# High and low activation parts of a projection as one 512-column product into a whole PSUM bank

## The chip, the cores and the metric

The kernel runs on one core of a Trainium2 chip. TensorE (PE) multiplies, VectorE (DVE), ScalarE (ACT) and GpSimd (POOL) do the rest of the arithmetic, SyncE (SP) issues most transfers. Each engine works through its own queue in order; semaphores tie the queues together. The metric is the device time of one execution in microseconds (us), the median over the runs.

## The reference, cut to what matters

256 tokens of width 1024 go through two layers of a first block (attention and a convolutional feed-forward network, FFN, each) and then through one hybrid layer. All of it is float32.

```
def conv_ffn(x, w_up, conv_w, conv_b, w_down):          # twice; FFN_HIDDEN = 2816
    u = x @ w_up                                        # [256, 5632]
    c = conv_b + sum of conv_w[j] * (u shifted by j - 1 tokens), j = 0..2
    g, val = c[..., :FFN_HIDDEN], c[..., FFN_HIDDEN:]
    return (jax.nn.gelu(g) * val) @ w_down

def hybrid_layer(x, ...):
    proj = rmsnorm(x) @ w_in
    (q_a, k_a, v_a, z_a, q_b, k_b, v_b, z_b, beta, decay, gate_a, gate_b) = split(proj)
    o_a = moba_attention(rope(q_a), rope(k_a), v_a)     # 8 heads; one block of 256 keys: causal attention
    y_a = (o_a * silu(z_a)) @ w_branch_a
    q_b, k_b, v_b = silu(causal_dwconv(concat(q_b, k_b, v_b)))
    o_b = gated_deltanet(q_b, k_b, v_b, g, beta)        # 8 heads
    y_b = (rmsnorm(o_b) * silu(z_b)) @ w_branch_b
    return x + rmsnorm((sigmoid(gate_a) * y_a + sigmoid(gate_b) * y_b) @ w_out)
```

`gated_deltanet` (GDN below) solves, in each head and each chunk of tokens, a triangular system of equations before its state can be carried on.

## The kernel before, in words

**Products in two parts.** PE multiplies in fp32r, and every operand of a weight product is split into a high part (rounded) and a low part (the rest). `mm3` (L130 to L133) issues three matmuls for one product: weights high by activations high (L131), weights high by activations low (L132), weights low by activations high (L133). Each loads its weights anew. In most projections the weights are the loaded operand, 128x128, and the 256 tokens stream as 256 columns; a projection sums eight k tiles. `wload` brings weights: SP issues the transfer (L110, five buffers), ACT rounds the high part (L116), DVE subtracts to get the low part (L117).

**PSUM.** A PSUM bank holds 512 float32 columns. Four banks are accumulators, tag "acc"; the four others are given out by tag in each layer: two "sm" and two "mm" in the FFN, one "sm", two "mm" and one "s" in the hybrid layer.

**The FFN** (L564) goes over 22 column tiles j. For j of 2 and more, two up products (gate and value half) are 16 `mm3` into the lower 256 columns of two banks; ACT and DVE read these banks for the three-tap convolution (L618, L619, L621), gelu follows, and the down product of an earlier j adds into the four accumulators with 512-column matmuls.

**The hybrid layer** (L734) is one function. Written order: v_a; beta and decay; the q_b and k_b projections of eight heads ("kq", `proj2`, L866, 16 `mm3` per head into one bank, alternately "acc" and "mm"), each followed by a four-tap convolution (L855), SiLU and the sum of squares on PE (`sumsq`, L876); from these sums reciprocal norms (from L898 on); the GDN matrices (L934, L937, L948 on PE, L952 and L954 on DVE, transposed by L927 and copied by L928); a round trip over DRAM and a substitution of 15 dependent steps (L973, L974) on DVE; v_b of four head pairs; three doubling levels (L1019, with L1029 and L1035 on DVE and the transposes L1038), for four systems each (two chunks, two groups of four heads); the outputs, four heads at a time (L1054, transposes L1059); then MoBA attention head by head (projection `h_qk`, copied out by ACT at L1102, scores L1110 to L1113, transposes L173, output L1134 and L1135) with the z projections (`zproj`, L1088); and last the gates and branches (L1174 on) and the output projection.

**What sets the order.** The written order is not the order of the queues. When the program is built, a scheduler orders the instructions of every engine and gives out the buffers; an instruction that takes a bank stands behind the release of that bank's last holder. So independent MoBA work, written behind GDN, is placed between GDN's steps where its banks allow it. The helper `behind` (L187) only adds such an order between two instructions. Before, the MoBA, z, gate and branch projections use "mm" banks (one each), and GDN's levels and outputs use "acc" banks (L923).

Of the kernel before, what the change touches and what calls it, by code (L numbers as in the profile page):

```python
# [17 lines left out]
P = 128  # L18
# [19 lines left out]
def build(tc, a, out):  # L38
# [15 lines left out]
    def banks(c2, **tags):  # L54
        """four banks of a layer, by tag; the other four are accumulators"""
# [44 lines left out]
    tsl = [slice(0, P), slice(P, 2 * P)]  # L100

    def wload(src, n, part=1024, tag="w", hb=HB, pool=None, eng=None, mk=None, scale=None):
        """a weight chunk [128, n]; returns its parts as (high, low) float32r tiles"""
# [30 lines left out]

    def small(n, dt=F32, tag=None):
        return xp.tile([P, n], dt, tag=tag or f"sm{n}", name=nm("s"), bufs=4 if n <= 8 else 1)
# [3 lines left out]
    def rsqrt(v, n, mul=1.0):  # L140
        """v [P, n] (all positive) -> mul/sqrt(v): bit guess, one tuned and one cubic step."""
# [21 lines left out]
        # y1 is -1/K1 of the first step's value  # L163
# [4 lines left out]
    def tposes(src_list, dst_hi, dst_lo=None, scale=None, eng="v", tag="sm"):  # L168
        """transpose [P,128] pieces into one bank, then move to dst ([P, n, 128] view)."""
# [17 lines left out]
    def behind(*ins):  # L187
        """what is traced here goes behind these instructions on their engines"""
# [13 lines left out]
    def newton(ss, n, width, ins=False, mid=None):  # L202
        """1/sqrt(mean(x^2)+eps) from the scaled sums of one or two parts: bit guess and two Newton
        steps, the first with tuned constants; the sums come scaled so that no factor is left over."""
# [27 lines left out]
    def postnorm(pool, tb, bnk, g_bc):  # L232
        """h += rmsnorm(y) g"""
# [13 lines left out]
    def postnorm_cut(pool, tb, cut, g_bc):  # L247
        """the same for the last token block, in pieces that go out as they are done"""
# [15 lines left out]
    def prenorm(tb, g_bc, aft, warm_):  # L264
        """xT = transpose(rmsnorm(h) g) as high and low parts; 1/rms enters through the transposing product"""
        ss = small(2, F32, "ss2")
        # without a gain here it is in the weights that follow
        hg = [xp.tile([P, 512], F32, tag=f"hg{tb}{f}", name=nm("hg"), bufs=1) if g_bc is not None else h[:, tb, hf[f]] for f in range(2)]
        for f in range(2):
            j_ = square(h[:, tb, hf[f]], D, ss, f)  # L270
            if warm_:
                # keeps the clock of the tensor engine up while it waits
# [30 lines left out]

    ends = []
    gate = []

    def boundary(accs, post, pre):
        """residual add of one sublayer and the norm of the next, a token block at a time;
        returns xT and what is left to do of it, by token block"""
        xT = None  # L310
        with npool() as pool:
# [5 lines left out]
            if pre:  # L317
                xT = [xp.tile([P, KT, S], F32R, tag=f"xT{i}", name=nm("xT"), bufs=1) for i in range(2)]
# [25 lines left out]
    def wide(src4, xT, bnk, mk=None, eng=None, hold=(), k0=4, cut=False):  # L344
        """generator: bnk[tb][f] = x @ w, w [1024, 1024] in four chunks of two k tiles; a step is one k tile
# [387 lines left out]
    def hybrid(xT, fin):  # L733
        with ExitStack() as c2:  # L734
# [125 lines left out]
            def big():  # L860
                cnt[0] += 1
                return acc() if cnt[0] % 2 else mmb()
# [465 lines left out]
```

## Time and profile before

| what | us |
|---|---|
| median of 3 runs | 1037.83 |
| lowest, highest | 1037.38, 1040.54 |
| span of the profiled execution | 1037.8 |
| PE busy in it | 1012.7 (98%) |
| DVE busy | 738.0 (71%) |
| ACT busy | 545.3 (53%) |
| HBM read | 160.08 MB, 156 GB/s |

The profiled execution's span is 1037.8 us, which is the median. PE's share is the first thing to look at; next, stage by stage, what DVE and ACT do beside it, and where in the hybrid layer PE's time goes to work that waits on other engines. The stages are, in the trace: FFN of layer 0 from about 150 us, FFN of layer 1 from about 480 us, the kq projections about 677 to 723 us, the GDN matrices and substitution to 795 us, levels and outputs 795 to 860 us, then MoBA and z, and the gates and branches about 910 to 1005 us.

### The profile page before, as it was taken

What the parts mean: (1) busy time and instruction counts of PE and PEld (TensorE: products, weight loads), DVE (VectorE), ACT (ScalarE), POOL (GpSimd) and SP (SyncE); (2) the same over time, 40 slices, a digit from 0 to 9 for tenths busy, and PEclk for the clock granted to TensorE, in tenths of its full rate; (3) what the DMA queues carried; (4) which work ended last, traced back from release to release, by engine and by line L of the source; (5) the groups of instructions that cost most, each with busy time, mean ns of one, the idle gap of its engine ahead of it and who ended that gap; (6) DMA issues with size and microseconds to landing.
All of it is one profiled execution on the core that took longest, in us unless ns stands there. A gap on an engine that the chain in (4) does not pass through costs nothing.

```text
span 1037.8 us, 18147 instructions
## 1 busy us (share of the span) xinstructions
PE 1012.7 (98%) x7120; PEld 924.6 (89%) x7120; DVE 738.0 (71%) x1387; ACT 545.3 (53%) x949; POOL 33.1 (3%) x35
## 2 busy tenths in 40 slices
PE   8889899999999999999999999999999999999997
PEld 6778799999987888799999998799898999999996
DVE  5775687777668479778777767578799657685563
ACT  5653466555436456557555554465554455544451
POOL 0000100000012000010000001000203000000000
PEclk9999999999999999999999999999999999999999
DMA  7562467555325425276655442444244413455541
GB/s 276 173 219 81 168 204 222 186 185 179 124 93 189 158 100 172 88 243 234 205 185 187 156 141 76 162 162 164 81 135 102 141 54 113 160 181 185 183 163 41
DMA packets 55301, 162.70 MB, mean 157 GB/s; under 512 B 12784, under 2 KB 15280, under 8 KB 55216
## 3 DMA queue, kind: packets, MB, share of 16 engines
q1 hardware_dynamic: 55216, 161.55, 47.4%
q8 instruction: 56, 0.92, 0.3%
q14 instruction: 29, 0.24, 0.1%
HBM read 160.08 MB, written 1.44 MB: 156 GB/s over the span
## 4 chain that ended last, share of the span: by engine, by line
PE 84%; DVE 9%; ACT 3%; DMA 2%; issue 1%; SPq 0%; POOL 0%; DVEq 0%; ACTq 0%; POOLq 0%
PE mm L131 11%; PE mm L132 11%; PE mm L133 11%; PE acc L132 8%; PE acc L131 8%; PE acc L133 8%; PE sm L133 4%; PE sm L132 4%; PE sm L131 4%; PE mm L583 2%; PE acc L1019 2%; DVE lo L117 1%; PE acc L1054 1%; PE s L699 1%; ACT junk L199 1%
## 5 line engine op out<-in xcount | busy, mean ns | idle before, releaser
L117 DVE TENSOR_TENSOR lo<-raw,hi 128x1024 fp32r<-128x1024 f32 (+1 forms) x271 | 326.5, 1208 | 140.6 <-ACT hi L116 139.4
L116 ACT CAST hi<-raw 128x1024 fp32r<-128x1024 f32 (+1 forms) x271 | 278.2, 1035 | 244.6 <-PE mm L132 126.6
L133 PE MATMUL mm<-xT,lo 128*128 128x256 f32 x928 | 265.6, 286 | 0.0
L131 PE MATMUL mm<-xT,hi 128*128 128x256 f32 x928 | 265.3, 286 | 0.0
L132 PE MATMUL mm<-xT,hi 128*128 128x256 f32 x928 | 264.9, 285 | 0.0
L132 PEld LDWEIGHTS mm<-xT,hi 128*128 128x128 f32 x928 | 177.6, 191 | 1.9 <-issue 0.7
L131 PEld LDWEIGHTS mm<-xT,hi 128*128 128x128 f32 x928 | 177.5, 191 | 1.5 <-issue 0.3
L133 PEld LDWEIGHTS mm<-xT,lo 128*128 128x128 f32 x928 | 177.6, 191 | 1.3 <-issue 0.7
L131 PE MATMUL sm<-xT,hi 128*128 128x256 f32 (+1 forms) x328 | 92.8, 283 | 0.0
L133 PE MATMUL sm<-xT,lo 128*128 128x256 f32 (+1 forms) x328 | 92.8, 283 | 0.0
L132 PE MATMUL sm<-xT,hi 128*128 128x256 f32 (+1 forms) x328 | 92.8, 283 | 0.0
L131 PE MATMUL acc<-hi,gv 128*128 128x512 f32 x176 | 69.2, 393 | 0.0
L132 PE MATMUL acc<-lo,gv 128*128 128x512 f32 x176 | 69.0, 392 | 0.0
L133 PE MATMUL acc<-hi,gv 128*128 128x512 f32 x176 | 68.5, 389 | 0.0
L132 PEld LDWEIGHTS sm<-xT,hi 128*128 128x128 f32 (+1 forms) x328 | 62.2, 190 | 0.9
L131 PEld LDWEIGHTS sm<-xT,hi 128*128 128x128 f32 (+1 forms) x328 | 62.2, 190 | 0.8
L133 PEld LDWEIGHTS sm<-xT,lo 128*128 128x128 f32 (+1 forms) x328 | 62.2, 190 | 0.1
L383 ACT ACTIVATE e<-s,s 128x256 f32<-128x256 f32 x46 | 21.5, 472 | 34.6 <-DVE s L380 32.8
L133 PEld LDWEIGHTS acc<-hi,gv 128*128 128x128 f32 x176 | 33.1, 188 | 7.5 <-DVE gv L125 0.3
L131 PEld LDWEIGHTS acc<-hi,gv 128*128 128x128 f32 x176 | 33.2, 189 | 6.3 <-ACT gv L125 0.6
L132 PEld LDWEIGHTS acc<-lo,gv 128*128 128x128 f32 x176 | 33.2, 189 | 5.3
L131 PE MATMUL mm<-og,hi 128*128 128x256 f32 x128 | 36.0, 281 | 0.0
(462 smaller groups left out, 1905.0 us busy)
## 6 DMA issues: line engine op xcount, KB each, us to landing
raw<-in_ffn_up SPq DMA_DIRECT2D x88, 512.0 KB, 4.6
raw<-in_ffn_down SPq DMA_DIRECT2D x44, 512.0 KB, 4.4
raw<-in_diff_qk SPq DMA_DIRECT2D x16, 512.0 KB, 5.2
raw<-in_h_kq SPq DMA_DIRECT2D x16, 512.0 KB, 4.5
raw<-in_h_qk SPq DMA_DIRECT2D x16, 512.0 KB, 3.9
raw<-in_h_z SPq DMA_DIRECT2D x16, 512.0 KB, 3.7
raw<-in_h_gate SPq DMA_DIRECT2D x16, 512.0 KB, 4.5
raw<-in_h_br SPq DMA_DIRECT2D x16, 512.0 KB, 4.6
```

The source lines that it names most:

```text
L116: nc.scalar.copy(hi[:, :k], raw[:, :k])
L117: (eng or nc.vector).tensor_tensor(lo[:, :k], raw[:, :k], hi.bitcast(F32)[:, :k], op=ALU.subtract)
L131: nc.tensor.matmul(o, l[0], r[0], start=start, stop=False)
L132: nc.tensor.matmul(o, l[0], r[1], start=False, stop=False)
L133: return nc.tensor.matmul(o, l[1], r[0], start=False, stop=stop)
L199: nc.scalar.activation(junk[:, :p.shape[-1]], p, AF.Square, scale=math.sqrt(beta_of(width)), accum_out=ss[:, i:i + 1])
L383: nc.scalar.activation(e[:, i], s_ps[:, i], AF.Exp, bias=mx[:, i:i + 1], scale=scale, accum_out=sm[:, i:i + 1])
L583: last = nc.tensor.matmul(mmf[j][:, t, tsl[tb]], raws[j][t][:, kt * P:kt * P + P], xF[kt // 4][:, kt % 4, tsl[tb]], start=kt == 0, stop=kt ...
L699: nc.tensor.matmul(sb, q[:, tsl[tb]], kb, start=True, stop=False)
L1019: nc.tensor.matmul(b[:, i], lhs(i), rhs(i), start=True, stop=True)
L1054: nc.tensor.matmul(b[:, i], lhs(hds[i], i), rhs(hds[i], i), start=True, stop=True)
```

## The change

A projection with 256 tokens now streams the high and the low activations as one 512-column matmul behind one load of the high weights, into the two halves of a bank, and the low weights times the high activations go on top of the first half. ACT copies the second half to SBUF and DVE adds the first half to it. High and low activations lie in one tile for this (`both`).

```diff
+    def mm2(o, l, r, start, stop):
+        nc.tensor.matmul(o, l[0], r, start=start, stop=False)
+        return nc.tensor.matmul(o[:, :S], l[1], r[:, 0], start=False, stop=stop)
+
+    def halves_sum(dst, o):
+        nc.scalar.copy(dst, o[:, S:])
+        return nc.vector.tensor_tensor(dst, o[:, :S], dst, op=ALU.add)
...
+    def both(pool, name, n):
+        t = pool.tile([P, 2, n, S], F32R, tag=name, name=nm(name), bufs=1)
+        return t[:, 0], t[:, 1], t
...
-                    b = [bank("mm" if j % 2 else "sm")[:, :S] for _ in range(2)]
+                    bs_ = [bank("mm" if j % 2 else "sm") for _ in range(2)]
                     for t in range(2):
                         for kt in range(KT):
-                            mm3(b[t], [w[:, kt * P:kt * P + P] for w in wu[t]], (xT[0][:, kt], xT[1][:, kt]),
-                                kt == 0, kt == KT - 1)
+                            mm2(bs_[t], [w[:, kt * P:kt * P + P] for w in wu[t]], xT[2][:, :, kt], kt == 0, kt == KT - 1)
+                    b = lp.tile([P, 2, S], F32, tag="u", name=nm("u"), bufs=2)
+                    for t in range(2):
+                        halves_sum(b[:, t], bs_[t])
+                    b = [b[:, t] for t in range(2)]
...
-            def big():
+            def two():
                 cnt[0] += 1
-                return acc() if cnt[0] % 2 else mmb()
+                return [mmb() if cnt[0] % 3 == 0 else acc() for _ in range(2)]
...
+            def projd(w, r=xd):
+                b_ = two()
+                for t in range(2):
+                    for kt in range(KT):
+                        last_mm[:] = [mm2(b_[t], [u[:, kt * P:kt * P + P] for u in w[t]], r(kt), kt == 0, kt == KT - 1)]
+                return b_
+
+            def added(b_, dst=None):
+                if dst is None:
+                    u_ = pair(0) if og[0] else lt("w5", [P, 4, P], bufs=6).rearrange("p (t b) s -> p t (b s)", t=2)
+                else:
+                    u_ = dst
+                for t in range(2):
+                    halves_sum(u_[:, t], b_[t])
+                return u_
...
-                b = proj2(wload(a["h_kq"][hd], 2048), big)
+                b = projd(wload(a["h_kq"][hd], 2048))
                 if pend is not None:
                     with behind(*last_mm):
                         sumsq(*pend)
+                b = added(b)
...
-                b = proj2(wload(a["h_z"][br, hp], 2048))
+                b = added(projd(wload(a["h_z"][br, hp], 2048)))
...
-                b = proj2(wload(a["h_qk"][hd], 2048))
-                qk = pair(0)
-                nc.scalar.copy(qk, b)
+                b = projd(wload(a["h_qk"][hd], 2048))
+                qk = added(b, pair(0))
...
-                    b = proj2(wload(a["h_gate"][br, mp], 2048))
+                    b = added(projd(wload(a["h_gate"][br, mp], 2048)))
...
-                    b = mmb().rearrange("p (t s) -> p t s", t=2)
-                    for t in range(2):
-                        for kt in range(KT):
-                            mm3(b[:, t], [u[:, kt * P:kt * P + P] for u in w[t]], (og[br][0][:, kt], og[br][1][:, kt]), kt == 0, kt == KT - 1)
+                    b = added(projd(w, lambda kt: og[br][2][:, :, kt]))
```

`mm3` stays in the attention of both layers, in v_a, v_b, beta and decay, in the down products and in the output projection. In the hybrid layer a projection now takes two banks, two "mm" at every third and two "acc" otherwise, where it took one. Lines move: L1019 of before is L1057 after, L1038 is L1076, L876 is L913, L934, L937 and L948 are L972, L975 and L986, L927 is L965; the two matmuls of `mm2` are L138 and L139.

The scheduler gives the queues a new order. The first place is PE behind the kq projections. Before, from the last matmul of the last kq projection on (mm_7854 is its bank, acc_7959 and acc_7986 hold GDN's decay matrices, acc_7972 and acc_7979 products of keys):

```order
L133 MATMUL mm_7854<-xT_6902,lo_7851 128x256
L876 MATMUL s_7296<-ones_7010,w_1537_7761 128x1 x4
L934 LDWEIGHTS idb_7008
L934 MATMUL acc_7959<-mG_7000,idb_7008 128x512
L937 MATMUL acc_7959<-h_triu_6992,gg_7278 128x128 x4
L948 MATMUL acc_7972<-QK_7295 128x256 x2
L948 MATMUL acc_7979<-QK_7295 128x256 x2
L934 LDWEIGHTS idb_7008
L934 MATMUL acc_7986<-mG_7000,idb_7008 128x512
L937 MATMUL acc_7986<-h_triu_6992,gg_7278 128x128 x4
L131 MATMUL mm_8177<-xT_6902,hi_8167 128x256
```

After, the same first GDN matrix (acc_7433) in its surroundings; mm_7732 is the bank of the second v_b pair, and 70 matmuls of v_b stand between the last kq matmul and this place:

```order
L132 MATMUL mm_7732<-xT_6457,hi_7722 128x256
L133 MATMUL mm_7732<-xT_6457,lo_7723 128x256
L131 MATMUL mm_7732<-xT_6457,hi_7722 128x256
L972 LDWEIGHTS idb_6562
L972 MATMUL acc_7433<-mG_6554,idb_6562 128x512
L975 MATMUL acc_7433<-h_triu_6546,gg_6832 128x128 x4
L986 MATMUL acc_7446<-QK_6849 128x256 x2
```

The first matrix stood directly behind the last kq matmul, and v_b (mm_8177) began behind two of them; now v_b's first pair and part of its second stand ahead of the first matrix, and the last sums of squares (L913) stand behind 96 v_b matmuls.

The second place is PE in the doubling levels. Before, one system and the start of the next (acc_8585 and acc_8591 are the level's two products, acc_8597 the transposes, mm_9250 is a projection of another part, s_9170 a MoBA head):

```order
L1038 MATMUL acc_8578<-c_ident,A_8153 128x128 x4
L1019 MATMUL acc_8585<-A_8153,M_7958 128x64 x4
L173 MATMUL sm_9165<-c_ident,ea_9153 128x128
L131 MATMUL mm_9250<-xT_6902,hi_9246 128x256
L132 MATMUL mm_9250<-xT_6903,hi_9246 128x256
L133 MATMUL mm_9250<-xT_6902,lo_9247 128x256
L131 MATMUL mm_9250<-xT_6902,hi_9246 128x256
L1019 MATMUL acc_8591<-w_1684_8584,VT_8154 128x64 x4
L1134 MATMUL s_9170<-pTa_9164,va_7022 128x256
L1135 MATMUL s_9170<-pTa_9164,va_7022 128x128
L1038 MATMUL acc_8597<-c_ident,A_8153 128x128 x4
L1019 MATMUL acc_8604<-A_8153,M_7958 128x64 x4
```

After, from the first level product on:

```order
L1057 MATMUL acc_7964<-A_7627,M_7432 128x64 x4
L1057 MATMUL acc_7970<-w_1714_7963,VT_7628 128x64 x4
L1076 MATMUL acc_7976<-c_ident,A_7627 128x128 x4
L1057 MATMUL acc_7983<-A_7627,M_7432 128x64 x4
L1057 MATMUL acc_7989<-w_1718_7982,VT_7628 128x64 x4
L1076 MATMUL acc_7995<-c_ident,A_7627 128x128 x4
L1057 MATMUL acc_8002<-A_7627,M_7432 128x64 x4
```

It goes on so for all 24 level products, the eight groups of transposes and the 16 groups of the outputs (two L1097, fourteen L1092): nothing of another part stands between them. Ahead of them stand, since the last kq matmul, the 192 matmuls of v_b, two `h_qk` projections of 32 matmuls each (mm_8305 and mm_8306, mm_8529 and mm_8530) and the scores of one head. The first z projection (acc_8389) and the other heads' `h_qk` projections follow behind the last output.

## Rows read from the trace of the kernel before

**Rows 1.** The page: busy time, share of the span, instructions.
```profile
PE 1012.7 (98%) x7120; PEld 924.6 (89%) x7120; DVE 738.0 (71%) x1387; ACT 545.3 (53%) x949; POOL 33.1 (3%) x35
```

**Rows 2.** Timeline of PE in the first FFN: start, duration, instruction.
```profile
200.96 0.40 PE L131 MATMUL acc<-hi,gv 128*128 128x512 f32 x1
...
203.71 0.28 PE L131 MATMUL sm<-xT,hi 128*128 128x256 f32 x1
...
205.98 0.28 PE L132 MATMUL sm<-xT,hi 128*128 128x256 f32 x1
```

**Rows 3.** Stretches: start:end, length, busy by engine, granted clock, DMA share, GB/s.
```profile
200.00:300.00 100.00, 100.00 (x717) 94.64 (x716) 70.24 (x107) 52.52 (x81) 0.00 (x0) 1.00 0.49 161
...
690.00:725.00 35.00, 35.00 (x298) 34.97 (x298) 28.92 (x48) 21.28 (x32) 0.00 (x0) 1.00 0.49 163
725.00:795.20 70.20, 67.06 (x523) 64.08 (x521) 63.01 (x162) 35.45 (x64) 10.32 (x6) 1.00 0.40 117
795.20:860.00 64.80, 64.79 (x557) 61.66 (x558) 40.40 (x84) 30.07 (x64) 3.29 (x1) 1.00 0.26 85
...
910.00:1005.00 95.00, 95.00 (x800) 95.00 (x799) 57.30 (x61) 43.11 (x50) 0.00 (x0) 1.00 0.55 184
```

**Rows 4.** Groups of ACT by form: a PSUM copy of 128x256.
```profile
L689 ACT COPY dq<-mm 128x256 f32<-128x256 f32 x8 | 3.0, 370 | 0.1
```

**Rows 5.** Groups of DVE by form: 128x256 with a PSUM source.
```profile
L1001 DVE TENSOR_TENSOR Vik<-sm,hik 128x256 f32<-128x256 f32 x8 | 3.3, 417 | 1.1 <-PE sm L1000 1.1
```

**Rows 6.** Stretches, instructions of L131 alone (PE, PEld), 725 to 795.2 us.
```profile
725.00:795.20 70.20, 38.38 (x134) 25.62 (x134) 1.00 0.40 117
```

**Rows 7.** The same, 795.2 to 860 us.
```profile
795.20:860.00 64.80, 16.58 (x56) 10.63 (x56) 1.00 0.26 85
```

**Rows 8.** Timeline of PE: end of the kq projections, first GDN matrix.
```profile
723.11 0.95 PE L876 MATMUL s<-ones,w 128*128 128x1 f32 x8
723.92 0.38 PE L934 MATMUL acc<-mG,idb 128*128 128x512 bf16 x1
...
725.02 1.89 PE L948 MATMUL acc<-QK 128*128 128x256 f32 x8
726.75 0.38 PE L934 MATMUL acc<-mG,idb 128*128 128x512 bf16 x1
```

**Rows 9.** Timeline of DVE: norms, first and last substitution step, level's first operand.
```profile
734.76 0.19 DVE L898 TENSOR_SCALAR vv<-s 128x32 f32<-128x32 f32 x1 [0.76 <-PE s L876]
...
766.57 0.15 DVE L973 TENSOR_TENSOR pr<-MB,TB 128x1 f32<-128x1 f32 x1
...
785.34 0.53 DVE L974 TENSOR_REDUCE TB<-pr 128x15 f32<-128x225 f32 x1
```

**Rows 10.** Timeline of PE: first level product, then level 2 and outputs.
```profile
795.17 1.10 PE L1019 MATMUL acc<-A,M 128*128 128x64 f32 x8 [1.80 <-DVE A L984]
...
834.19 0.68 PE L1019 MATMUL acc<-A,M 128*64 128x64 f32 x8
...
836.19 0.68 PE L1019 MATMUL acc<-A,M 128*64 128x64 f32 x8
...
838.18 0.66 PE L1059 MATMUL acc<-c_ident,QK 128*128 128x128 f32 x4
...
848.48 0.60 PE L1059 MATMUL acc<-c_ident,QK 128*128 128x128 f32 x4
```

**Rows 11.** Timeline of DVE: first step of three successive systems.
```profile
819.31 0.42 DVE L1029 TENSOR_TENSOR w<-acc,h_lmask 128x256 f32<-128x256 f32 x1 [1.59 <-PE acc L1019]
...
826.58 0.42 DVE L1029 TENSOR_TENSOR w<-acc,h_lmask 128x256 f32<-128x256 f32 x1
```

**Rows 12.** Timeline of PE around a wait in layer 0.
```profile
66.22 0.50 PE L131 MATMUL acc<-hi,oT 128*128 128x512 f32 x1 [1.81 <-ACT oT L125]
```

**Rows 13.** Stretches behind that wait, columns as in rows 3.
```profile
68.00:72.00 4.00, 4.00 (x15) 3.26 (x15) 1.43 (x6) 2.07 (x5) 0.00 (x0) 0.61 0.45 143
72.00:76.00 4.00, 3.88 (x24) 3.38 (x23) 2.88 (x6) 1.52 (x6) 0.00 (x0) 1.00 0.41 130
```

More of the change, by code (lines that the diff above doesn't have):

```diff
@@ L317, in boundary @@
             if pre:
-                xT = [xp.tile([P, KT, S], F32R, tag=f"xT{i}", name=nm("xT"), bufs=1) for i in range(2)]
+                xT = both(xp, "xT", KT)
             last = []
@@ L496, in w_o @@
                             hd == 0, hd == H - 1)
-            slots = iter(("xT0", "xT1"))
+            slots = []
             def spare():
-                t = xp.tile([P, 2, 1024], F32R, tag=next(slots), name=nm("xo"), bufs=1)
-                return t[:, 0], t[:, 1]
+                if not slots:
+                    t = xp.tile([P, 4, 1024], F32R, tag="xT", name=nm("xo"), bufs=1)
+                    slots.extend((t[:, 2 * i], t[:, 2 * i + 1]) for i in range(2))
+                return slots.pop(0)
             scale = 192 ** -0.5
@@ L787, in hybrid @@
             x2 = lambda kt: (xT[0][:, kt], xT[1][:, kt])
+            xd = lambda kt: xT[2][:, :, kt]
             vbs = [[acc(), acc()] for _ in range(2)]
@@ L1151, in hybrid @@
             for br in range(2):
-                og[br] = [lt(f"og{br}{i}", [P, H, S], F32R) for i in range(2)]
+                og[br] = both(gp_, f"og{br}", H)
             for hp in range(4):
@@ L1190, in hybrid, with spare2 @@
             bs = [[acc(), acc()], [(acc(), 0, 512), (acc()[:, :256], 512, 256), (mmb()[:, :256], 768, 256)]]
-            slots = iter(("og00", "og01", "og10", "og11"))
-            run(wide(a["h_out"], mg, bs, mk=spare, cut=True))
+            left, n_og = [], iter(range(2))
+            def spare2():
+                if not left:
+                    t = lt(f"og{next(n_og)}", [P, 4, 1024], F32R)
+                    left.extend((t[:, 2 * i], t[:, 2 * i + 1]) for i in range(2))
+                return left.pop(0)
+            run(wide(a["h_out"], mg, bs, mk=spare2, cut=True))
             boundary(bs, ("post_g", 0), None)
```

## The prediction, made before the changed kernel ran

> **What bounds the kernel now.** I read the page first, then the stretches, then the order of the queues. On the page PE is busy 98% of the span [rows 1]; in the stretches it is busy without a gap in the FFN and in the gates, at a granted clock of 1.00 [rows 3]. So a matmul saved there comes off the end. The stretch to look at longest is 723 to 860 us. In it stands the one long dependent chain of the kernel: norms, GDN matrices, a DRAM round trip, 15 substitution steps on DVE, three levels, outputs. Yet PE is idle for only 3.1 us between 725 and 795.2 us and not at all between 795.2 and 860 us [rows 3], because work of other parts stands between the chain's steps. Whether that work is still there is as important as the price of a matmul.
>
> **The saving on PE.** Back to back, twelve 512-column matmuls go from 200.96 to 203.71 us, 0.2292 us each; the next nineteen 256-column ones take from 203.71 to 205.98 us, 0.1195 us each [rows 2]. A 512-column matmul is thus 9.8 ns shorter than two of 256 columns. `mm3` costs 3 x 0.1195 = 0.358 us, `mm2` 0.229 + 0.1195 = 0.349 us. The change replaces 2 x 20 x 16 = 640 `mm3` in the FFNs and (8 + 8 + 8 + 8 + 8) x 16 = 640 in the hybrid layer (kq, qk, z, gates, branches). 1280 x 9.8 ns = 12.5 us, 6.3 of it in the FFNs. The starts are rounded to 0.01 us, which leaves 11 to 14 us.
>
> The trace has 0.2292 and 0.1195 us, that is about 10 ns beside what scales with the columns [rows 2]. The Trainium skill ("TensorE: Matmul & The Clock Gate", section "Back-to-back issue gap") gives a gap of the columns over 2.4 GHz and some 2.5 ns for an isolated warm matmul. By that rule the saving would be 2.5 ns x 1280 = 3.2 us. The measured pitches decide; the rule's result stands as a rival below.
>
> **What it adds on ACT and DVE.** Each half projection gets one ACT copy of 128x256 from PSUM, 0.37 us as at L689 [rows 4], and one DVE add of that size, 0.42 us as at L1001 [rows 5]: per FFN tile 0.74 and 0.83 us. A tile takes PE 48 x 0.1195 + 12 x 0.2292 = 8.5 us. DVE is at 70% there and goes to 80% of it, ACT from 53 to 62% [rows 3]; that hides, and if it did not, a tile would cost at most the 0.83 us, 33 us in all. The add queues on DVE behind the ACT copy of its half, and the weight splits queue behind the add; with 20% spare I take it at nothing. At the gates DVE has 57.3 of 95 us [rows 3] and gets 16 x 0.83 = 13 us more: hidden. In kq it is tight: 28.9 of 35 us [rows 3], 6.1 heads, 6.1 x 0.83 = 5.1 us more, against 34.4 us of PE: full. I take nothing there, with 0 to 3 us kept in the range. The old copy of 512 columns at L1102 goes; two copies of 256 take its place.
>
> **What it moves.** This is where the forecast is made. The projections of heads take two "acc" banks in two cases of three. The chain uses "acc" too. In the new order PE has, between the last kq matmul and the first level product, v_b, two qk projections and one head's scores, and behind it nothing but the chain until the last output. In the order of before, 56 `mm3` stand between the levels and outputs [rows 7], 20.1 us, and the scores of several heads.
>
> First, the time up to the levels. kq ends at 723.1 us [rows 8]; after, 128 x 9.8 ns earlier, 721.8. Work of PE from there to the first level: v_b 64 x 0.358 = 22.9 us; the two qk projections 32 x 0.349 = 11.2 us; the rest as before: 67.1 us busy [rows 3] less 133 `mm3` (L131 has 134 matmuls [rows 6]), 47.7 us, is 19.4 us, and 1.9 us between 723.1 and 725.0. Sum 55.4 us. When does the level start? Before, the last sum of squares is read at 734.76 us, the substitution runs from 766.57 to 785.9 us [rows 9], the first level at 795.17 us [rows 10]. In the new order 96 v_b matmuls, 11.5 us, two decay groups at 1.1 us, two key groups at 0.9 us [rows 8] and the sums themselves, 1.2 us, precede it: PE is through at 738 us at the earliest, and at 742 if it waits for weights or a bank on the way, 4 to 8 us later than before. The substitution, 19.3 us long with DVE's other work in between [rows 9], may get 2 to 3 us back from fewer heads beside it. The first level then comes at 797 to 803 us; I take 799. The SP transfers of this round trip move with it; the weight loads queued behind them serve projections that now come later anyway. From 721.8 to 799 us are 77.2 us, less 55.4 is 21.8 us of idle PE, 18.7 more than the 3.1 of before. Bounds: 13.6 if the level isn't delayed at all (795.2 - 1.3), 22.7 at 803.
>
> Second, the chain by itself. A level step of one system: the DVE steps of successive systems stand 7.27 us apart for two [rows 11], 3.63 us each, in a place with little between them and DVE mostly idle; eight systems are 29.1 us. The last level takes 2.0 us per system [rows 10], four are 8.0 us. An output group takes 10.3 us from its transposes to the next one's, with pieces of a MoBA head in it [rows 10]; I take 9.3 without them, twice, 18.6 us. Sum 55.7 us. PE's own share of it, from the pitches of the same stretch: 64.8 us less 20.1 us of `mm3` [rows 3, 7] and some 9 us of scores, about 36 us. So PE is idle for 20 us, where it was idle for none. Bounds: 14 if the steps close up to 50 us, 24 if the outputs stay at 10.3 and the systems at 3.9 us. The work that stood there isn't gone; it comes behind the last output, where PE is full.
>
> Sum for the forecast: 1037.8 - 12.5 + 18.7 + 20 = 1064 us, and 2 us for the clock behind the long wait (next part): **1066 us**, 2.7% slower.
>
> **Rivals.** *The gaps do no harm.* If PE's order costs less than the saving, the kernel is faster. Mechanism: the chain's steps close up so far that it is bound by PE's own 36 us, and the projections ahead of it last until the first level. It decides at 12.5 us of new idle time; with none, 1037.8 - 12.5 = 1025 us. For it: DVE does its step of 0.42 us quickly, and in the old order some of the 3.63 us may be the matmuls put between. Against it: each product waits for a DVE step and each DVE step for a product, in a queue in order; the bounds above together are 27.6 us at least. A result within 0.3% (3 us, about what a measurement of this kernel can tell from no change) would need these sums to cancel.
>
> *The clock.* After a wait of 1.81 us before 66.22 us [rows 12] the granted clock was 0.61 over 68 to 72 us, the lower of its levels (1.2 of 2.4 GHz) for most of it, and 1.00 again after that [rows 13]: 4 us x 0.39 = 1.6 us lost. Behind a longer wait, in a chain with gaps of about a microsecond, it may stay low. If half of the chain's 36 us run at the lower level, they cost 18 us more: 1064 + 18 = 1082 us. Against it: between 725 and 795 us there are waits of up to 1.8 us [rows 10] and the clock stays at 1.00 [rows 3]. The skill's same page, section "HAM oscillation — how this bites in real kernels", says that idle gaps bring the array back to the low clock; the trace agrees at 68 us, and shows no case of a longer gap.
>
> *The fixed share isn't saved.* If three quarters of the 10 ns belong to something that a 512-column matmul pays as well, the saving is 3 us in place of 12.5: 1066 + 9 = 1075 us. Rows 2 speak against it: both sizes are measured back to back with a load each [rows 2]. The gap rule of the skill, above, comes to this result.
>
> *More is saved, or less lost.* With both idle bounds at the low end and the saving at 14 us: 1037.8 - 14 + 27.6 = 1051 us; if DVE interleaves the substitution better too, some 1045 us.
>
> *It doesn't do what it says:* the scheduler keeps 512-column matmuls waiting for whole banks in the FFN. There each tile takes two banks of a tag before and after, and they are let go earlier; I see no case for it.
>
> **How the numbers follow.** Forecast and its bounds (1051 to 1075): 0.68, the case of the fixed share included with 0.04. Clock: 0.14, 1075 to 1090. Less lost, 1041 to 1051: 0.08. Within 3 us of before: 0.04. Faster, 1025 to 1034: 0.06. The range from 1046 to 1084 leaves out the faster and equal cases, half of the less-lost case and a part of the clock's, about 2 in 10. Faster 0.06, same 0.04, slower 0.90.
>
> **What would show it.** Right: the FFN stretches shorter by about 3.1 us each, PE without a gap in them; a long idle of PE ahead of L1057, several us in one piece; PE about 65% busy from the first L1057 to the last L1092, with waits for DVE and ACT; full again behind it. Wrong: PE full in that stretch; an FFN tile longer than 8.4 us, which would make DVE the bound; a pitch of the 512-column matmul with a 256-column one that isn't 0.349 us; or a granted clock of 0.5 through the levels, which is the second rival.

## The result, and the profile after

The changed kernel takes 1103.41 us (median of 4, 1102.52 to 1106.41) against 1037.96 us: 1.063 times the time before, interval 1.0613 to 1.0647. The direction was foretold, the size was not: 65 us, where 28 were forecast and the range ended at 1084 us.

The page of the changed kernel: busy time, then PE's busy tenths and the granted clock in 40 slices of 27.5 us.

```profile
PE 1037.5 (94%) x5840; PEld 884.5 (80%) x5840; DVE 789.4 (72%) x1547; ACT 591.3 (54%) x1101; POOL 30.6 (3%) x35
...
PE   8899899999999999999999999988658799999997
...
PEclk9999999999999999999999999998955799999999
```

Beside [rows 1] PE has 1280 matmuls fewer (5840 for 7120) and is busy for 25 us *more*. Fewer matmuls can only be busy longer if each takes longer: the clock line says where, in slices 28 to 32, about 743 to 880 us.

The hybrid layer in stretches with the same meaning in both kernels: from the first sum of squares to the end of the first projections, on to where the last sum of squares is read, to the first level product, to the end of the outputs, to the end. Columns as in [rows 3]. First the kernel before:

```profile
689.90:723.10 33.20, 33.20 (x282) 33.20 (x282) 27.86 (x47) 19.86 (x30) 0.00 (x0) 1.00 0.48 161
723.10:734.80 11.70, 11.70 (x96) 11.35 (x95) 7.32 (x13) 6.29 (x12) 0.42 (x1) 1.00 0.29 91
734.80:795.20 60.40, 57.26 (x446) 54.61 (x445) 56.85 (x151) 30.58 (x54) 9.90 (x6) 1.00 0.43 124
795.20:860.20 65.00, 64.99 (x559) 61.86 (x560) 40.60 (x84) 30.07 (x64) 3.29 (x1) 1.00 0.26 85
860.20:1037.80 177.60, 170.86 (x1343) 165.47 (x1341) 109.86 (x174) 80.18 (x116) 0.00 (x0) 0.99 0.45 149
```

Then the changed kernel, with the levels (807.5 to 866) and the outputs (866 to 887) apart, and a stretch of the first FFN ahead of them:

```profile
200.00:300.00 100.00, 99.89 (x525) 84.91 (x525) 77.14 (x134) 60.89 (x109) 0.00 (x0) 1.00 0.44 153
682.60:718.20 35.60, 33.95 (x194) 29.26 (x192) 26.31 (x45) 19.46 (x31) 0.00 (x0) 0.95 0.42 150
718.20:746.80 28.60, 22.34 (x156) 21.26 (x154) 19.56 (x38) 16.05 (x33) 0.62 (x1) 0.91 0.31 111
746.80:807.50 60.70, 43.40 (x248) 36.76 (x248) 47.39 (x138) 21.45 (x43) 7.91 (x6) 0.84 0.28 83
807.50:866.00 58.50, 47.12 (x228) 42.63 (x229) 9.92 (x17) 7.60 (x16) 2.15 (x1) 0.50 0.00 0
866.00:887.00 21.00, 16.41 (x123) 15.14 (x122) 8.58 (x13) 7.43 (x13) 0.00 (x0) 0.95 0.01 2
887.00:1100.00 213.00, 206.72 (x1184) 178.55 (x1183) 160.30 (x297) 114.99 (x211) 0.00 (x0) 0.99 0.43 151
```

Up to the first sum of squares the changed kernel is 7.3 us ahead (682.6 for 689.9). In the hybrid layer it loses 69.8 us (417.7 for 347.9). Two columns account for it. PE idle, length less busy: 47.5 us after, 9.9 before, so 37.6 us more. And PE busy at less than full clock, busy times (1 - clock) summed over the rows from 682.6 to 887 us: 1.7 + 2.0 + 6.9 + 23.6 + 0.8 = 35 us, where before has none there. 37.6 + 35 - 69.8 leaves 2.8 us for the saving of 640 shorter pairs. The two columns are an account, not two separate prices: a PE at half clock also fills time in which it would otherwise have waited.

One level step of a system, timeline of PE in the changed kernel:

```profile
807.52 1.97 PE L1057 MATMUL acc<-A,M 128*128 128x64 f32 x8 [6.58 <-DVE A L1022]
811.22 1.94 PE L1057 MATMUL acc<-w,VT 128*128 128x64 f32 x8 [1.72 <-DVE w L1067]
813.67 1.11 PE L1076 MATMUL acc<-c_ident,A 128*128 128x128 f32 x4 [0.51 <-DVE A L1073]
814.58 1.81 PE L1057 MATMUL acc<-A,M 128*128 128x64 f32 x8
816.90 1.97 PE L1057 MATMUL acc<-w,VT 128*128 128x64 f32 x8 [0.52 <-DVE w L1067]
819.39 1.12 PE L1076 MATMUL acc<-c_ident,A 128*128 128x128 f32 x4 [0.52 <-DVE A L1073]
820.29 1.81 PE L1057 MATMUL acc<-A,M 128*128 128x64 f32 x8
```

A wait of 6.58 us stands ahead of the first product. From then on no work of another part stands between the steps, and each product takes 1.8 to 2.0 us where it took 1.1 [rows 10]. A step is 814.58 to 820.29, 5.71 us, for 3.63 before [rows 11]. From the transposes on the waits between are only 0.5 us each: at the low clock PE itself is the longer part of the chain.

And the chief waits of PE between 676 and 812 us (in total, times, longest):

```profile
PE s L913 <- ACT w L930: 7.6, 4, 3.0
PE acc L1057 <- DVE A L1022: 6.6, 1, 6.6
...
PE sm L183 <- ACT ea L1166: 3.6, 1, 3.6
...
PE mm L138 <- ACT hi L116: 2.1, 2, 1.1
```

Behind the wait for `ea`, which ends at 797.6 us, the clock is at 0.50, well ahead of the first level product:

```profile
798.00:804.00 6.00, 2.37 (x7) 1.47 (x6) 1.71 (x4) 0.48 (x1) 0.00 (x0) 0.50 0.54 116
```

The first wait of the list is not in the kernel before: `sumsq` on PE waits for ACT's squares in the kq stage.

### The profile page after: what moved, and what is told of

The parts are those of the page before. It is cut to its first block, busy times and chain, and to the rows that moved or that the text cites. A ratio compares the mean times of both kernels' runs of the same rounds, so it can differ in the third digit from the quotient of the medians.

```text
span 1100.3 us, 15875 instructions
## 1 busy us (share of the span) xinstructions
PE 1037.5 (94%) x5840; PEld 884.5 (80%) x5840; DVE 789.4 (72%) x1547; ACT 591.3 (54%) x1101; POOL 30.6 (3%) x35
## 4 chain that ended last, share of the span: by engine, by line
PE 81%; DVE 10%; ACT 3%; issue 2%; DMA 2%; SPq 0%; POOL 0%; DVEq 0%; ACTq 0%
PE mm L138 11%; PE acc L138 9%; PE sm L138 7%; PE acc L132 6%; PE acc L131 6%; PE acc L133 6%; PE mm L139 5%; PE acc L139 5%; PE sm L139 3%; PE acc L1057 3%; PE mm L600 2%; DVE lo L117 2%; PE mm L131 2%; PE mm L132 2%; PE mm L133 2%
## 5 line engine op out<-in xcount | busy, mean ns | idle before, releaser
L138 PE MATMUL mm<-xT,hi 128*128 128x512 f32 x496 | 178.3, 400 | 2.1 <-ACT hi L116 2.1
L139 PE MATMUL mm<-xT,lo 128*128 128x256 f32 x496 | 141.6, 286 | 1.7 <-DVE lo L117 1.7
L138 PE MATMUL acc<-xT,hi 128*128 128x512 f32 x336 | 122.2, 404 | 0.1
L138 PE MATMUL sm<-xT,hi 128*128 128x512 f32 x320 | 113.9, 399 | 0.0
L138 PEld LDWEIGHTS mm<-xT,hi 128*128 128x128 f32 x496 | 93.9, 189 | 23.9 <-ACT hi L116 2.6
L139 PEld LDWEIGHTS mm<-xT,lo 128*128 128x128 f32 x496 | 94.5, 191 | 4.1 <-DVE lo L117 2.7
L139 PE MATMUL acc<-xT,lo 128*128 128x256 f32 x336 | 95.9, 286 | 0.0
L139 PE MATMUL sm<-xT,lo 128*128 128x256 f32 x320 | 90.0, 281 | 0.0
L138 PEld LDWEIGHTS acc<-xT,hi 128*128 128x128 f32 x336 | 64.2, 191 | 14.1 <-issue 0.2
L138 PEld LDWEIGHTS sm<-xT,hi 128*128 128x128 f32 x320 | 60.3, 188 | 14.5
L131 PE MATMUL acc<-hi,gv 128*128 128x512 f32 x176 | 69.3, 394 | 0.1
L139 PEld LDWEIGHTS acc<-xT,lo 128*128 128x128 f32 x336 | 64.5, 192 | 0.4
L139 PEld LDWEIGHTS sm<-xT,lo 128*128 128x128 f32 x320 | 60.6, 189 | 0.7
L133 PE MATMUL mm<-xT,lo 128*128 128x256 f32 x160 | 47.3, 295 | 0.0
L132 PE MATMUL mm<-xT,hi 128*128 128x256 f32 x160 | 47.0, 294 | 0.0
L131 PE MATMUL mm<-xT,hi 128*128 128x256 f32 x160 | 46.8, 292 | 0.1
```

The costliest lines, as they stand in the source:

```text
L131: nc.tensor.matmul(o, l[0], r[0], start=start, stop=False)
L132: nc.tensor.matmul(o, l[0], r[1], start=False, stop=False)
L133: return nc.tensor.matmul(o, l[1], r[0], start=False, stop=stop)
L138: nc.tensor.matmul(o, l[0], r, start=start, stop=False)
L139: return nc.tensor.matmul(o[:, :S], l[1], r[:, 0], start=False, stop=stop)
```

## The experiments

Behind each measured time stands its ratio to the kernel before, as it ran beside that experiment, with the 95% interval; it is taken over the runs of both and isn't the quotient of two medians. The median of the kernel before was 1038.4 to 1040.9 us there.

**What shuts the other work out.** Behind the change, two things are shared between GDN's chain and the projections that used to stand between its steps: accumulator banks (`two`), and the ring of six w5 tiles, from which `added` takes z's sum and GDN its intermediate results. Three kernels undo the one, the other, both.

The banks alone:

```diff
+            def mm2b():
+                return [mmb(), mmb()]
...
-                b_ = two()
+                b_ = (bk or two)()
...
+                b = projd(wload(a["h_qk"][hd], 2048), bk=mm2b)    # so too z, gates, branches
```

> The changed kernel, with one thing different: the projections behind kq (qk, z, gates, branches) take their two banks from the mm pair always, never from the four accumulators. Theory A (a projection is shut out of the GDN chain by either of two shared things, an accumulator bank or the ring of sum tiles that z shares with GDN): the ring still holds the first z back, its two mm banks stay taken, so PE's order through the chain stays empty and the time stays near the changed kernel's 1103 us: 1092 to 1112. Rival B (the accumulator banks alone do it): work returns between the levels, 1035 to 1055 us. Rival C (the added ACT copies and DVE adds do it): also 1092 to 1112, but then the run with both things undone is slow too.

Measured: 1111.53 us, 1.0668 (1.0625 to 1.071), 8 us more than the changed kernel. The levels, in its stretch of the trace, are as in the changed kernel:

```profile
807.30:866.00 58.70, 47.28 (x229) 42.78 (x230) 9.94 (x17) 7.60 (x16) 2.17 (x1) 0.50 0.00 0
```

The ring alone:

```diff
+                if og[0] is None:
+                    b_ = projd(wload(a["h_z"][br, hp], 2048))
+                    th = pair(1)
+                    for t in range(2):
+                        zu = lp.tile([P, S], F32, tag="zu", name=nm("zu"), bufs=1)
+                        halves_sum(zu, b_[t])
+                        nc.scalar.activation(th[:, t], zu, AF.Tanh, scale=0.5)
+                        nc.vector.scalar_tensor_tensor(th[:, t], th[:, t], 1.0, zu, op0=ALU.add, op1=ALU.mult)
+                    return th
```

> The changed kernel with only z's sum in a tile of its own; the banks as in the change. Theory A: the first z projection and the next head still wait for accumulators that GDN holds, so the chain stays empty: 1092 to 1112 us. Rival D (the ring of sum tiles alone does it): 1035 to 1055 us.

Measured: 1102.15 us, 1.0576 (1.0532 to 1.0619): nothing is gained.

Both edits together:

> The changed kernel with both shared things taken away: mm banks alone for the projections behind kq, and z's sum in a tile of its own, half by half. The matmuls of the change and all its copies and adds are kept. Theory A: projections stand between the level products again, PE is over 95% busy and its clock 1.00 from the first level product to the last output; what stays lost is the waiting in kq and before the levels. 1030 to 1055 us, 1042 the likeliest. Rival C (added copies and adds): still above 1085 us.

Measured: 1063.13 us, 1.0201 (1.016 to 1.0241). From the first level product to the outputs its trace shows:

```profile
810.80:878.00 67.20, 66.05 (x494) 60.16 (x493) 40.29 (x86) 28.91 (x64) 1.51 (x1) 0.94 0.16 57
```

494 matmul records in place of some 350, PE 98% busy, the clock back up. Either thing alone keeps the projections out; only without both does the work return, and 40 us with it. The prediction named the banks alone, which would have been wrong as a remedy. Rival C falls as the cause of the main loss, since this kernel has all the copies and adds. But 1063 is 21 us over the likeliest value and 8 us over the range, and the clock is 0.94, not 1.00.

**The kq stage.** The next two kernels put kq back to three matmuls, one bank and no adds:

```diff
-                b = projd(wload(a["h_kq"][hd], 2048))
+                b = proj2(wload(a["h_kq"][hd], 2048), big)
...
-                b = added(b)
```

> Both shared things taken away as in e2_both, and the kq projections as before: three matmuls, one bank, no copies and adds. Theory: what is left of the loss in e2_both (24 us) comes from kq, where a sum of squares on PE waits for ACT's square, which stands behind a weight cast that waits for PE (7.6 us in four waits in the changed kernel, and the clock low behind them). Then nothing is left of the loss and the saving shows: 4.3 us in the FFNs and 512 x 7 ns = 3.6 us in the hybrid layer, 7.9 us under the kernel before. 0.990 to 0.996 of it. Rival (the new order or the adds of qk and z still cost): 1045 us and more.

> The changed kernel with only kq as before; banks and ring of sum tiles shared as in the change. The levels stand back to back again. If the waits in kq add to those of the levels, 24 us less than the changed kernel: 1075 to 1085. If they are taken up by the wait for the levels, since PE has too little to do ahead of them in either case, 1095 to 1104.

Measured: with both shared things gone 1047.45 us, 1.0082 (1.0058 to 1.0106); with them shared 1083.84 us, 1.0437 (1.0408 to 1.0465). The four kernels make a square:

| | shared banks and ring | both undone |
|---|---|---|
| kq changed | 1103.4 | 1063.1 |
| kq as before | 1083.8 | 1047.5 |

The shut-out costs 36 to 40 us and kq 16 to 20 us, and within 4 us they add: what PE loses in kq is not taken up by the wait that follows. With the shared things kept, the stretch from the first level product to the end of the levels is as in the changed kernel, only 20 us earlier. The row of the stretch, and the first two products (L1060 is L1057 there):

```profile
787.20:845.60 58.40, 46.34 (x229) 41.84 (x230) 11.34 (x19) 7.99 (x17) 2.11 (x1) 0.51 0.03 9
...
787.17 1.10 PE L1060 MATMUL acc<-A,M 128*128 128x64 f32 x8 [1.28 <-DVE A L1025]
...
790.88 1.94 PE L1060 MATMUL acc<-w,VT 128*128 128x64 f32 x8 [2.43 <-DVE w L1070]
```

The first product still takes 1.10 us, the second 1.94: here no wait of 6.6 us stands ahead, and the clock is at 0.51 all the same.

Putting kq back undoes more than its copies and adds. Its matmuls, its banks and the order behind it go back as well: PE begins the GDN matrices directly behind the last kq projection again, and with the shared things kept the last sum of squares is read at 728.0 us, for 747.0 in the changed kernel. The 16 to 20 us are the price of all this together.

What PE waits for in kq shows in two timelines of the changed kernel, PE and then ACT (start, length, instruction, wait):

```profile
709.80 1.05 PE L913 MATMUL s<-ones,w 128*128 128x1 f32 x8 [1.55 <-ACT w L930]
710.96 0.75 PE L138 MATMUL acc<-xT,hi 128*128 128x512 f32 x1
711.72 0.63 PE L138 MATMUL acc<-xT,hi 128*128 128x512 f32 x1
712.36 0.63 PE L138 MATMUL acc<-xT,hi 128*128 128x512 f32 x1
...
708.17 1.04 ACT L116 CAST hi<-raw 128x1024 fp32r<-128x1024 f32 x1 [1.25 <-PE acc L138]
709.13 0.62 ACT L930 ACTIVATE w<-QK 128x512 f32<-128x512 f32 x1
```

PE waits for a square; ACT's queue has that square behind the cast of a weight chunk, and the cast waits for PE to give a buffer back. The kernel before has no wait of PE for a square in kq. That two copies and two adds per head, which lengthen the turn through ACT and DVE, close this circle fits, but is argued: no run takes them away alone. Behind the wait of 1.55 us, 512-column matmuls stand 0.64 us apart (pairs, 711.72 to 712.36), for 0.35 at full clock.

With kq as before and both things undone, the expectation was 8 us *under* the kernel before; the measured time is 8 to 9 us over it. PE's waits from 735 to 860 us in that kernel (L1063 is the level product, L143 the added sum of two halves):

```profile
PE acc L1063 <- DVE w L1073: 2.6, 1, 2.6
PE mm L138 <- DVE zu L143: 1.8, 1, 1.8
PE acc L1063 <- DVE A L1028: 1.5, 1, 1.5
PE mm L138 <- DVE pr L876: 1.5, 1, 1.5
```

Its clock is 0.94 and 0.93 in the stretches of GDN's preparation and levels. DVE is 90% busy in the preparation (48.1 of 53.3 us; 56.85 of 60.4 in the kernel before), and the sums of qk and z come on top just there. That fits the waits; no run separates it, so this last part stays argued.

**The clock as a cost of its own.** The changed kernel, with PE kept busy in the chain's waits:

```diff
-                        nc.tensor.matmul(b[:, i], lhs(i), rhs(i), start=True, stop=True)
+                        last_ = nc.tensor.matmul(b[:, i], lhs(i), rhs(i), start=True, stop=True)
+                    with behind(last_):
+                        j_ = smb()
+                        for _ in range(3):
+                            nc.tensor.matmul(j_, idb, mG[:, None, :].to_broadcast([P, 4, P]), start=True, stop=True)
```

> The changed kernel with three more 512-column bf16 matmuls (0.22 us each at full clock) behind each of the 24 level products, into a bank that nobody reads: PE is kept busy in the waits for DVE and ACT, nothing else is different. If the low clock is a cause of its own (granted 0.50 from 798 to 866 us in the changed kernel, a level step of a system 5.7 us where 3.6 were foretold), the clock returns to 1.00 soon after the first products, a step takes some 4 us, and 1103 falls to 1082 to 1095 us. If the waits alone set the length of the chain, it stays at 1100 to 1112 us, or gets longer by up to 72 x 0.22 = 16 us.

Measured: 1089.83 us, 1.0483 (1.0452 to 1.0514), 13.6 us less with 72 matmuls more. The levels:

```profile
809.60:853.00 43.40, 42.95 (x293) 29.85 (x293) 9.85 (x17) 7.22 (x15) 2.10 (x1) 0.91 0.00 1
```

43.4 us for some 57.5 us (807.5 to 865), at a clock of 0.91 for 0.50. The low clock is thus a cost by itself, 14 us of this chain. The edit also moved something that the expectation didn't see: the transposes of the one head scored ahead of the levels ask for the same "sm" bank and now stand in the outputs, and PE's wait ahead of the first product is 13.4 us, for 6.6. The levels gain all the same, with nothing but the added matmuls between their steps.

**The FFNs alone, and the pitch of a pair.** The hybrid layer as before, the rest of the change kept:

> The change in the two FFNs alone; the hybrid layer as before. From the pitch of a pair in the trace of the changed kernel (0.3527 us against 3 x 0.1198 = 0.3594 us before) 640 pairs save 4.3 us: 1033.6 us, 1032 to 1036. By the prediction's pitch (9.8 ns a pair) 6.3 us: 1031.6. If the copies and adds cost time in the FFN, 1037 or more.

Measured: 1039.35 us beside 1039.41, ratio 0.9989 (0.9963 to 1.0015). No difference in the time. The executions differ in their mean clock, 0.991 to 0.999 in both kernels, which makes 8 us. Span times mean clock, a rough measure of the time at full clock, has a median of 1030.6 us for this kernel and 1034.0 for the one before: 3.4 us less, as the pitch has it. In its profile the clock is low from 790 to 800 us, behind a wait of 1.9 us ahead of the first level product; the first half of it:

```profile
790.00:795.00 5.00, 4.27 (x24) 4.01 (x23) 4.17 (x7) 1.05 (x1) 1.73 (x1) 0.57 0.12 50
```

The saving is there in the pitch, and that the clock took it back in these executions fits the two medians; no run holds the clock fixed.

The pitch itself, timeline of PE in the FFN of the changed kernel; fifteen pairs lie between the two rows:

```profile
200.29 0.28 PE L139 MATMUL sm<-xT,lo 128*128 128x256 f32 x1
...
205.59 0.28 PE L139 MATMUL sm<-xT,lo 128*128 128x256 f32 x1
```

5.30 us for 15 pairs is 0.3533 each; over the two FFNs the mean is 0.3527, and three 256-column matmuls before took 3 x 0.1198. A pair saves 6.7 ns, not 9.8. Is it that the 512 columns lie in two stretches?

```diff
-        t = pool.tile([P, 2, n, S], F32R, tag=name, name=nm(name), bufs=1)
-        return t[:, 0], t[:, 1], t
+        t = pool.tile([P, n, 2, S], F32R, tag=name, name=nm(name), bufs=1)
+        return t[:, :, 0], t[:, :, 1], t
```

> The change in the FFNs alone, as in the run of that name, but with the high and low activations of a k tile side by side, so that the 512 columns of the long matmul are one contiguous stretch (before: two stretches of 256 columns, 8 KB apart). If the two stretches make the pair 0.3527 us long in place of the 0.3487 of the prediction, the pair falls to 0.349 in the FFN, 640 x 4 ns = 2.6 us of the time. If a pair of unlike matmuls costs that by itself, its pitch stays at 0.352 to 0.353 and the time is that of the run before, within 2 us.

Measured: 1039.32 us, 1.0000 (0.9982 to 1.0018), and the same pitch in its trace. It isn't the layout. Is it the order of the sizes?

```diff
                         for kt in range(KT):
-                            mm2(bs_[t], ...)
+                            nc.tensor.matmul(bs_[t], wu[t][0][:, kt * P:kt * P + P], xT[2][:, :, kt], start=kt == 0, stop=False)
+                        for kt in range(KT):
+                            nc.tensor.matmul(bs_[t][:, :S], wu[t][1][:, kt * P:kt * P + P], xT[0][:, kt], start=False, stop=kt == KT - 1)
```

> The change in the FFNs alone, with the matmuls of a projection in another order: first the eight of 512 columns, then the eight of 256 columns. If it is the alternation of sizes that makes a pair 0.3527 us long, the streams take 0.229 and 0.1195 us each and the sum of a pair falls to 0.349: 2.5 us less than with the FFNs alone. If a 512-column matmul of this kind (activations streamed) is longer by itself, its pitch in its stream is 0.233 or more and the time is that of the FFNs alone.

Measured: 1034.66 us beside 1040.94, ratio 0.9953 (0.9932 to 0.9973); span times clock 1029.3 us for 1034.7. Its timeline of PE:

```profile
200.76 1.98 PE L628 MATMUL sm<-xT,hi 128*128 128x512 f32 x8
202.57 1.12 PE L630 MATMUL sm<-xT,lo 128*128 128x256 f32 x8
203.53 2.00 PE L628 MATMUL sm<-xT,hi 128*128 128x512 f32 x8
205.37 1.12 PE L630 MATMUL sm<-xT,lo 128*128 128x256 f32 x8
```

Eight long ones take 1.81 us, eight short ones 0.96 us (200.76, 202.57, 203.53): 0.346 a pair. In the FFN the grouped order is some 7 ns a pair shorter than the alternating one, and with it the change in the FFNs beats the kernel before by half a per cent.

But alternation alone isn't the cause. In the changed kernel's own trace whole projections of the hybrid layer alternate at the short pitch. One of kq, at a granted clock of 1.00, with eight pairs from the first row to the second:

```profile
677.02 0.39 PE L138 MATMUL mm<-xT,hi 128*128 128x512 f32 x1
...
679.79 0.39 PE L138 MATMUL mm<-xT,hi 128*128 128x512 f32 x1
```

That is 2.77 us, 0.346 a pair; others, as the seven pairs from 705.26 to 707.74 us, take 0.354. What decides between the two pitches no run shows.

**Behind the chain.** FFNs, gates, branches and the late z changed, on mm banks; kq, qk and the early z as before:

> The change where nothing waits for a projection in a chain: the FFNs, the gates, the branches and the late z, all on mm banks; kq, qk and the early z as before. 640 pairs in the FFNs and 320 behind the chain at 7 ns are 6.7 us of PE. In the run with the FFNs alone the saving of 4.3 us did not show in the time, and its trace has the granted clock at 0.57 behind the wait for the first level product (790 to 800 us), which costs 3 to 7 us. Theory (saving real, clock takes it back): 1032 to 1040 us, and the span times the mean clock some 6 us below that of the kernel before. Rival (no saving on PE at all): span times clock as before.

Measured: 1039.43 us beside 1040.94, 0.9993 (0.9977 to 1.0009). Span times clock is 1032.7 us for 1034.7, a gain of 2.0 us where some 6 were expected and the FFNs alone gave 3.4. The 320 pairs behind the chain bring nothing that shows; why, no run tells.

**Filling the wait ahead of the levels.** Four fp32 matmuls on what the substitution leaves:

```diff
+            j_ = smb()
+            for _ in range(4):
+                nc.tensor.matmul(j_[:, :256], ident, TBt.rearrange("p a b -> p (a b)"), start=True, stop=True)
             V = lt("A", [P, 2, H, P])
```

> As e9_late_only, with four fp32 matmuls of 256 columns (1.7 us together) in the wait ahead of the first level product, on data that the substitution leaves and into a bank that nobody reads. Theory: PE's wait there, 1.8 us in the kernel before, closes, the clock stays at 1.00 behind it, and the saving shows: 1030 to 1034 us. Rival: the low clock there comes from other waits too, or the four matmuls delay the level: as e9_late_only or slower.

> The kernel before with the same four matmuls ahead of the first level product and nothing else. The mean clock of the kernel before was 0.995 to 0.998 in its runs beside the experiments, 2 to 5 us. If that is lost behind this wait, 1034 to 1037 us; if elsewhere (layer 0 has a wait of its own at 64 to 66 us), 1037 to 1040 us.

Measured: 1057.9 us (1.0168, 1.0149 to 1.0187) and 1061.8 us (1.0204, 1.0184 to 1.0223). 1.7 us of work costs 18 us beside the run without it and 21 us beside the kernel before. There is one "sm" bank in this layer; the transposes of the attention heads need it, and those written later now stand behind these four matmuls, which wait for the substitution. The same four matmuls in an accumulator, `j_ = acc()`, which no head uses there:

> The kernel before with the same four matmuls in an accumulator. If the wait there lowers the clock, 1036 to 1038 us at a mean clock of 0.998 or more; if elsewhere, 1038 to 1041 at 0.996. If it comes out near 1060 as with the sm bank, the four matmuls themselves delay the level, and it wasn't the bank.

> The grouped FFN version (1034.7 us, span times clock 1029) with four fp32 matmuls, 1.7 us, ahead of the first level product, into an accumulator. If the wait there lowers the clock in some executions, the mean clock rises to 0.998 or 0.999 in all of them, and the median falls to 1030 to 1033 us. If the clock falls elsewhere, it stays at 0.995 to 0.997 and 1034 to 1036 us.

Measured: the kernel before with it 1041.95 us (1.002, 1.0004 to 1.0036), the grouped FFN version 1034.83 us (0.9952, 0.9932 to 0.9972). So it was the bank, not the work. The stretch from 735 us to the first level product, on the kernel before, first in the "sm" bank and then in an accumulator:

```profile
735.00:783.80 48.80, 36.70 (x258) 33.18 (x256) 38.60 (x102) 16.63 (x31) 7.94 (x5) 0.92 0.40 116
...
735.00:795.00 60.00, 57.07 (x436) 54.00 (x435) 56.49 (x149) 30.58 (x54) 9.56 (x5) 1.00 0.43 125
```

With the shared bank PE is 75% busy at a clock of 0.92, with the other 95% at 1.00. The first level product even comes earlier with the shared bank, at 783.8 us; what the kernel lost is the work that stood beside the chain (258 matmuls in this stretch for 436). Four matmuls in the wrong buffer repeat the effect of the change in small. As a remedy for the clock the filling failed: the median of the mean clocks is 0.997 in both runs, 0.996 in the kernel before beside them, and the grouped version's profile has the clock low at 35, 70 and 795 us.

## Why the prediction was wrong

**The step that failed is the clock.** The sum took 2 us for it and put the case of a clock that stays low at 0.14, priced at 18 us. In the account above it is 35 us: the clock is 0.50 through all the levels, 23.6 us of it, and between 0.84 and 0.95 in the 125 us ahead of them. Of this 13.6 us are shown by a run, the one that kept PE busy in the levels. That rival had the right mechanism, evidence in [rows 12, 13], and was wrong in two ways. It was priced for half of the chain, while behind waits of 1.5 us in kq the clock was low too; and the evidence against it, waits of 1.8 us with the clock at 1.00 [rows 3, 10], was one execution: with the FFNs alone changed, a wait of 1.9 us at the same place has 0.57 behind it. Nor does it take the long wait that the prediction set the 2 us for: with kq as before the levels are at 0.51 behind waits of 1.28 and 2.43 us. A sparse chain is another case, and the kernel before has none to read it from. The sentence of the Trainium skill ("TensorE: Matmul & The Clock Gate", section "HAM oscillation — how this bites in real kernels") that idle gaps bring the array back to the low clock agrees with this run: 0.50 from 798 us, behind the wait of 3.6 us for `ea`, to about 866 us. That it stayed there with waits of only 0.5 us between the products is read from this run alone.

**Idle time: right in sum, by luck.** 18.7 + 20 us were foretold, 37.6 measured. Ahead of the levels it is 22.1 (1.65 + 6.26 + 17.3 - 3.1). In levels and outputs it is 16 (11.4 + 4.6), though these take 79.5 us in place of the 55.7 foretold: PE is busy for 63.5 us of them, not 36, most of it at half clock. Two errors cancel. The first level came at 807.5, not at 797 to 803 us: the last sum of squares was read at 747.0, where PE was to be through with it at 738 to 742, and from there to the level it is as long as before (60.7 us for 60.4).

**kq, taken at nothing, cost 16 to 20 us.** This is the second step that failed. The prediction saw DVE full there and kept 0 to 3 us. It counted busy time against PE's time and not the turn of one head through ACT and DVE, on which PE's in-order `sumsq` waits. What is queued behind what was missing: the square behind the cast, the cast behind PE. Without this loss the kernel takes 1083.8 us, still 18 over the forecast, and its first level comes at 787.2 us, earlier than any bound of the prediction.

**The saving: 6.7 ns a pair, not 9.8.** The pitches of [rows 2] are those of streams of one size. Grouped by size the pair takes 0.346 us, 3 ns less than foretold from them; alternating it takes 0.353 in the FFN and 0.346 to 0.354 in the hybrid layer.

**The place was right, the cause half right.** The projections did fall behind the chain, as the order showed. That accumulators are the reason was argued from the code; the ring of sum tiles does it too, and each suffices.

**The adds hide in the FFN:** DVE 77%, ACT 61% with PE at 99.9%, close to the 80 and 62% foretold.

## What to carry to other kernels

Ask of every buffer that a change takes from a shared tag what asks for it earlier in written order and how long that holder keeps it: one bank or tile that a long chain also uses can push all independent work behind that chain, and a count of matmuls doesn't see it. Where PE goes from full to sparse, price the stretch at half the clock as well as at full, since one execution of a full kernel doesn't show which it will be. And in a stage where an engine's queue waits in order for another's result, follow one item's turn through all queues; busy shares below 100% prove nothing there.

## What the runs showed of the hardware

Matmuls of 512 and 256 columns that alternate, each with its own weights, took 0.353 us a pair in the FFN; eight of one and then eight of the other took 0.346 us a pair, with the activations in two stretches in both. In the hybrid layer some alternating projections took 0.346 and others 0.354. Putting the 512 columns side by side changed nothing. Seventy-two matmuls that nobody reads, put among a sparse chain, made its levels 14 us shorter, at a granted clock of 0.91 for 0.50. That chain stood at 0.50 with waits of half a microsecond between products that kept PE 81% busy.
